# Decode tokens of a hybrid decoder layer: outputs from the old recurrent state, new state made in a later stage

## The chip, the cores and the metric

One core of one Trainium2 chip runs the whole step. The metric is device time in microseconds (us) of one execution; the figure to compare is the median of three runs.

## The reference

One decoder layer is applied to a prompt of 1024 tokens and to 8 decode tokens (one new token for each of 8 sequences). Both go through a half-step SwiGLU feed-forward, then attention heads beside Mamba-2 heads, an output projection, cross attention into 256 memory tokens, a second half-step feed-forward and a final norm. The part that matters here is the Mamba-2 recurrence of a decode token. For every sequence, head and channel, with the old state h0 (128 numbers per channel), it computes

```
h = exp(dt * a) * h0 + dt * x * B        # 16 heads x 64 channels x 128, an output
y = sum over n of C[n] * h[n] + d_skip * x
```

All of h (8 x 16 x 64 x 128 floats, 4 MB) is an output, and y goes on through the gate, the group norm and the output projection of the same layer. B and C are shared by the 8 heads of a group; there are two groups.

## The kernel before

Activations lie with features on the 128 partitions and the 1032 tokens along the free dimension. Matrix products are made of three fp32r products of a high and a low part. Tensors come from pools of slots by tag: a tile waits until its slot is free, which is when the last user of the tile that held it, a DMA included, is done. The order of instructions on each engine comes from a scheduler, which walks the program with a cost model and takes, for each engine, the first instruction in program order that is ready; so an instruction can run far ahead of its place in the program, and its order against others is fixed before the run. Nearly all DMAs are issued by one in-order queue, SyncE's (SPq).

The stages are, in order of time in the profile: first feed-forward (to about 860 us), attention with the input projections as filler (to 1310), the scan (1310 to 1545), the output projection (to 1640), cross attention (1640 to 1860), the last projection and preparation (to 1965), second feed-forward.

In the scan, `ssd(g, c)` (L1200) handles chunk c of group g of the prompt: it loads a 128 x 1024 row block `bc` (L1206), takes exponentials on ScalarE (L1210, L1212, L1217), multiplies on VectorE (L1227) and GpSimd (L1229, L1240, L1258), multiplies on TensorE (L1241, L1250) and adds the state on VectorE (L1259). Beside it run the z projections (`pzz`), the first half of the output projection (`wout_o`, L1368: load 344 columns, multiply, add, store back), gates and splits (`gate_split`, L1295). The decode tokens have their place between the chunks. `dec_conv(g)` (L1308) makes x, B, C and dt * x; `dec_ssm(g, b0)` (L1335) handles two sequences; `dec_out(g)` (L1353) adds the skip term and copies the result to the last 8 columns. In `dec_ssm`, a pair of states `sv` sits in one slot of the tag "hb", which has three slots and is shared with `bc`; `t1` is a PSUM bank (PS) of the pair that `pst` of `ssd` uses too.

Cross attention is `cross_q(h)` (query projection, TensorE), `cross_att(h)` (prompt) and `cross_dec(h)` (decode tokens, with 8 loads of 512 KB of cached keys and values per head) for four heads; `cross_in` loads back stored outputs, and from L1672 the last projection `pco` runs as filler. `sq_` and `acc_` are rings of 4 and 3 slots of 388 columns (tags "tu" and "ts").

Of the kernel before, what the change touches and what calls it, by code (L numbers as in the profile page):

```python
# [10 lines left out]
F32 = mybir.dt.float32  # L11
F32R = mybir.dt.float32r
I32 = mybir.dt.int32
AF = mybir.ActivationFunctionType
OP = mybir.AluOpType
# [4 lines left out]
NDEC = 8  # L20
# [56 lines left out]
def tile_step(ctx, tc, a, o):  # L77
    nc = tc.nc
    pool = lambda **kw: ctx.enter_context(tc.tile_pool(**kw))
    cp = pool(name="consts", bufs=1)  # L80
# [5 lines left out]
    st = {}  # L86
# [23 lines left out]
    sq_, acc_, g1_, u1_ = ring("tu", 4, PA), ring("ts", 3, PA), ring("tg", 2, PA), ring("tv", 2, 344)  # L110
# [33 lines left out]
    def PS(name="ps"):  # L144
        return st["pair"].tile(list(st["shape"]), F32, name=name, tag="s", bufs=st["bufs"])
# [717 lines left out]
    def conv_block(m):  # L863
# [7 lines left out]
        def ev(p, s, n):  # L871
# [15 lines left out]
            def rows():  # L887
                q = PD("pcv")
                nc.tensor.transpose(q[:11, :128], tail, ident)
                cvo = tq.tile([16, 128], F32, name="cvo", tag="cvo", bufs=1)[:11]  # L890
                nc.scalar.copy(cvo, q[:11, :128])
                nc.sync.dma_start(o[4][0, 0][:, m * 128:(m + 1) * 128], cvo[0:3])
                nc.sync.dma_start(o[10][0, :, 2, m * 128:(m + 1) * 128], cvo[3:11])
# [37 lines left out]
    for t0, n in TGS:  # L931
        s = slice(t0, t0 + n)
        p = PD("pdt")
# [370 lines left out]
    ct = mp.tile([128, 6, NDEC], F32, name="ct")  # L1304
    dtx = [mp.tile([128, 4, NDEC], F32, name=f"dtx{g}") for g in range(2)]
    yd = [mp.tile([128, 4, NDEC], F32, name=f"yd{g}") for g in range(2)]

    def dec_conv(g):  # L1308

# [22 lines left out]
        nc.vector.tensor_copy(bcT, flat(p)[:8, :256])  # L1332
        nc.sync.dma_start(bc_scr[g], bcT)

    def dec_ssm(g, b0):  # L1335

        sv = H("hb", "sv")[:, :1024].rearrange("p (b j n) -> p b j n", b=2, n=128)
        hs = slice(g * 8, g * 8 + 8)
        for u in range(2):
            b = b0 + u  # L1340
            nc.sync.dma_start(sv[:, u], a["state_ssm"][0, b, hs].rearrange("(j e) p n -> (e p) j n", e=2))
            bb = acc_()[:, :256]
            nc.sync.dma_start(bb, bc_scr[g, b:b + 1].broadcast_to([128, 256]))
            t1 = PS("pt1").rearrange("p (j n) -> p j n", n=128)
            for j in range(4):
                nc.scalar.activation(t1[:, j], bb[:, :128], AF.Copy, scale=dtx[g][:, j, b:b + 1])
                nc.scalar.activation(sv[:, u, j], sv[:, u, j], AF.Copy, scale=ddb[:, 1, g * 4 + j, b:b + 1])
            nc.vector.tensor_add(sv[:, u], sv[:, u], t1)
            nc.vector.tensor_mul(t1, sv[:, u], bb[:, None, 128:].to_broadcast([128, 4, 128]))
            nc.vector.tensor_reduce(yd[g][:, :, b], t1, mybir.AxisListType.X, OP.add)  # L1350
            nc.sync.dma_start(o[11][0, b, hs].rearrange("(j e) p n -> (e p) j n", e=2), sv[:, u])

    def dec_out(g):  # L1353
        nc.vector.tensor_mul(dtx[g], xcd[:, g, 0:4], dsk[:, g * 4:g * 4 + 4, None].to_broadcast([128, 4, NDEC]))
        nc.vector.tensor_add(yd[g], yd[g], dtx[g])
        for j in range(4):
            nc.vector.tensor_copy(xc[4 * g + j][:, SEQ:T], yd[g][:, j])
# [286 lines left out]

    cross_q(0)
    cross_q(1)
    cross_att(0)
    cross_dec(0)
    cross_q(2)
    cross_att(1)  # L1650
    cross_dec(1)
    cross_q(3)
    for k in range(4):
        cross_in(k)
    acts[4:] = [(A("coh"), A("col")) for _ in range(4)]
    cross_dec(2)
    cross_att(2)
    cross_dec(3)
    cross_att(3)
    wco = lambda half, m: w_co[half * 512:half * 512 + 512].rearrange("(k p) n -> p k n", p=128)[:, :, m * 128:(m + 1) * 128]  # L1660
    x = [None] * KD

# [174 lines left out]
```

## Time and profile before

| what | value |
| --- | --- |
| median of three runs | 2673.5 us (2665.6 to 2675.37) |
| the profiled execution | 2677.61 us, of it 2675.8 us from its first to its last instruction |
| VectorE, ScalarE, GpSimd busy | 67%, 44%, 34% of the span |
| mean granted TensorE clock | 0.972 of full speed |
| HBM | 204.25 MB read, 49.98 MB written |

TensorE is busy nearly throughout. A stage is judged by how far TensorE falls short in it and by what TensorE then waits for; the averages over the span say little about a stage.

### The profile page before, as it was taken

Reading aid. Unit: us, or ns where it says so; the run is one execution under the profiler, and the core shown is the slowest. Engines: PE = TensorE matmul, PEld = TensorE weight load, DVE = VectorE, ACT = ScalarE, POOL = GpSimd, SP = SyncE. Lnnn points to the kernel's source line nnn. Section 1 sums busy time; section 2 is a strip of 40 time slices with the busy share of each in tenths; the row PEclk is TensorE's granted clock in tenths of the full one; section 3 lists DMA queues with packets and bytes.
Section 4 is the critical chain, followed back from the end, with each engine's and each line's share of the span. In section 5 each row is a group of like instructions: output and inputs, shape, how many; then the busy total and the mean of one; then the engine's idle time right before and its main releaser. Section 6 shows DMA issues by size and latency. Waiting matters only on the chain.

```text
span 2675.8 us, 42135 instructions
## 1 busy us (share of the span) xinstructions
PE 2517.3 (94%) x15999; PEld 2391.8 (89%) x15999; DVE 1797.9 (67%) x3648; ACT 1172.5 (44%) x2413; POOL 911.8 (34%) x687
## 2 busy tenths in 40 slices
PE   6899999999999999999897899989889999999998
PEld 5899999999998899999686798879789999999997
DVE  7566666666667676778578867565686666666665
ACT  5433333333334455554477523232443333333345
POOL 5433333333325111115265664101643333333333
PEclk9999999999999999999898999999999999999999
DMA  5411211112113222227666634573111111111112
GB/s 171 136 49 57 62 60 57 57 57 64 57 48 105 75 69 78 87 74 236 199 196 221 211 94 134 170 219 116 34 48 48 48 48 49 55 48 51 53 48 80
DMA packets 273748, 252.13 MB, mean 94 GB/s; under 512 B 17392, under 2 KB 243880, under 8 KB 273536
## 3 DMA queue, kind: packets, MB, share of 16 engines
q1 hardware_dynamic: 271872, 249.34, 30.3%
q8 instruction: 126, 2.06, 0.3%
q14 instruction: 78, 0.64, 0.1%
q10 hardware_dynamic: 1672, 0.09, 0.0%
HBM read 204.25 MB, written 49.98 MB: 95 GB/s over the span
## 4 chain that ended last, share of the span: by engine, by line
PE 69%; DVE 14%; DMA 8%; issue 3%; ACT 3%; POOL 2%; SPq 0%; DVEq 0%; ACTq 0%; POOLq 0%
PE fb L319 44%; PE pqkv L255 5%; PE pxbc L255 4%; PE pcq L255 2%; PE pco L255 2%; DMA fraw<-in_w_up_dram 2%; PE pwa L255 2%; PE po L1061 1%; DVE fs L353 1%; PE ps L1035 1%; PE ptr L1055 1%; PE pzz L255 1%; DMA cqb<-cq_scr 1%; DVE ckv L1531 1%; DMA kb<-in_cache_win_k_dram 1%
## 5 line engine op out<-in xcount | busy, mean ns | idle before, releaser
L245 POOL TENSOR_TENSOR wl<-wr,wh 128x1024 fp32r<-128x1024 f32 (+4 forms) x79 | 165.5, 2095 | 569.9 <-ACT wh L241 542.4
L307 POOL TENSOR_TENSOR fw<-fraw,fw 128x512 fp32r<-128x512 f32 x131 | 174.7, 1333 | 467.4 <-ACT fw L306 387.8
L307 POOL TENSOR_TENSOR fw<-fs,fw 128x512 fp32r<-128x512 f32 x128 | 172.5, 1348 | 398.6 <-ACT fw L306 351.0
L306 ACT CAST fw<-fs 128x512 fp32r<-128x512 f32 x256 | 158.2, 618 | 272.6 <-PE fb L319 161.3
L306 ACT CAST fw<-fraw 128x512 fp32r<-128x512 f32 x262 | 162.2, 619 | 186.2 <-PE fb L319 182.2
L353 DVE TENSOR_TENSOR fs<-fraw 128x512 f32<-128x512 f32 (+1 forms) x168 | 103.4, 615 | 136.0 <-DMA fraw<-in_w_up_dram 67.3
L307 DVE TENSOR_TENSOR fw<-fraw,fw 128x512 fp32r<-128x512 f32 x131 | 102.2, 780 | 113.0 <-ACT fw L306 113.0
L307 DVE TENSOR_TENSOR fw<-fs,fw 128x512 fp32r<-128x512 f32 x128 | 96.2, 752 | 94.4 <-ACT fw L306 94.4
L319 PE MATMUL fb<-hRh,fw 128*128 128x256 f32 x640 | 137.3, 280 | 0.4
L241 ACT CAST wh<-wr 128x1024 fp32r<-128x1024 f32 (+1 forms) x80 | 76.8, 960 | 117.8 <-PE pwa L255 29.7
L319 PEld LDWEIGHTS fb<-hRh,fw 128*128 128x128 f32 x640 | 109.2, 188 | 3.6 <-DVE x L505 3.6
L255 PE MATMUL pxbc<-xh,wh 128*128 128x344 f32 x288 | 94.0, 326 | 2.0 <-DVE xr L872 2.0
L255 PE MATMUL pqkv<-xh,wh 128*128 128x344 f32 x288 | 93.8, 326 | 0.3 <-DVE x L535 0.3
L255 PE MATMUL pxbc<-xl,wh 128*128 128x344 f32 x288 | 93.5, 325 | 0.0
L255 PE MATMUL pqkv<-xh,wl 128*128 128x344 f32 x288 | 93.1, 323 | 0.0
L255 PE MATMUL pqkv<-xl,wh 128*128 128x344 f32 x288 | 92.9, 323 | 0.0
L255 PE MATMUL pxbc<-xh,wl 128*128 128x344 f32 x288 | 92.9, 323 | 0.0
L319 PE MATMUL fb<-hRl,fw 128*128 128x256 f32 x320 | 87.7, 278 | 0.0
L398 DVE TENSOR_TENSOR tu<-fb,ts 128x388 f32<-128x388 f32 x44 | 24.7, 562 | 90.2 <-ACT ts L395 90.2
L1042 ACT ACTIVATE pr<-pr,nm 128x128 f32<-128x128 f32 (+3 forms) x64 | 49.7, 777 | 55.3 <-DVE nm L1040 55.0
L319 PE MATMUL fb<-T2h,fw 128*128 128x388 f32 x160 | 54.2, 359 | 18.7 <-ACT fb L488 18.7
L1040 DVE CUSTOM_DVE_ANT_0 pr<-ps,U 128x128 f32<-128x128 f32 (+3 forms) x64 | 48.1, 751 | 27.2 <-PE ps L1035 16.9
(806 smaller groups left out, 9420.3 us busy)
## 6 DMA issues: line engine op xcount, KB each, us to landing
fraw<-in_w_gate_dram SPq DMA_DIRECT2D x44, 512.0 KB
fraw<-in_w_up_dram SPq DMA_DIRECT2D x44, 512.0 KB
fraw<-in_w_down_dram SPq DMA_DIRECT2D x44, 512.0 KB
wr<-in_w_in_dram SPq DMA_DIRECT2D x32, 512.0 KB
x_scr<-x SPq DMA_DIRECT2D x16, 516.0 KB
x<-x_scr SPq DMA_DIRECT2D x16, 516.0 KB
bc<-acs_scr SPq DMA_DIRECT2D x16, 512.0 KB
ckv<-in_cache_mem_k_dram SPq DMA_DIRECT2D x16, 512.0 KB
```

What stands on the lines that cost most here:

```text
L241: nc.scalar.copy(hi[:, :w], raw[:, :w])
L245: e.tensor_sub(lo[:, q], raw[:, q], hi[:, q].bitcast(F32))
L255: nc.tensor.matmul(ps, w, v, start=i == 0, stop=i == last)
L306: nc.scalar.copy(hi, src)
L307: (nc.vector if st["turn"] else nc.gpsimd).tensor_sub(lo, src, hi.bitcast(F32))
L319: nc.tensor.matmul(ps, l[:, js], m, start=bool(start and not i), stop=bool(stop and i == 2), skip_group_check=True)
L353: nc.vector.tensor_tensor(dst, t[p], t[q], op=op)
L1035: ins = nc.tensor.matmul(ps[:, c:c + n], qs[:, b * 128:w], kk[:, c:c + n], start=i == 0, stop=i == 1)
L1040: nc.vector.tensor_tensor_reduce(pr[:, :w], ps[:, :w], U[:, 896 - b * 128:1024], -1.0, 3e38, OP.add, OP.min, nm)
L1042: nc.scalar.activation(pr[:, :w], pr[:, :w], AF.Exp, scale=-1.0, bias=nm, accum_out=sm)
L1055: nc.tensor.transpose(p[:, j], pr[:, (c + j) * 128:(c + j + 1) * 128], ident)
L1061: nc.tensor.matmul(po[:, b % 2].rearrange("p i t -> p (i t)"), vv[:, j, e].rearrange("p i d -> p (i d)"), tts[j // 4][:, j % 4].rearrange( ...
```

## The change

`dec_ssm` no longer makes the new state. It multiplies the loaded old state by C on GpSimd, in place, sums over n on VectorE, and takes the product B.C of each token with one more VectorE instruction. `dec_out` then scales these sums by exp(dt * a) and adds (dt * x) * (B.C); it also keeps copies of dt * x and exp(dt * a) that outlive the scan. A new function, `dec_state(g, b)`, loads the old state of one sequence a second time, loads B, makes h on ScalarE and GpSimd and stores it; sixteen calls of it are placed between the calls of the cross attention. A small tile, `cvo`, moves from a slot of its own to the ring "tu".

```diff
-                cvo = tq.tile([16, 128], F32, name="cvo", tag="cvo", bufs=1)[:11]
+                cvo = sq_(128)[:11]
...
+    dab = cp.tile([128, 8, NDEC], F32, name="dab")
+    dtb_ = [cp.tile([128, 4, NDEC], F32, name=f"dtb{g}") for g in range(2)]
...
+    bC = [mp.tile([128, NDEC], F32, name=f"bC{g}") for g in range(2)]
+    rows8 = lambda t, g, b: t[0, b, g * 8:g * 8 + 8].rearrange("(j e) p n -> (e p) j n", e=2)
+
     def dec_ssm(g, b0):
 
         sv = H("hb", "sv")[:, :1024].rearrange("p (b j n) -> p b j n", b=2, n=128)
-        hs = slice(g * 8, g * 8 + 8)
         for u in range(2):
             b = b0 + u
-            nc.sync.dma_start(sv[:, u], a["state_ssm"][0, b, hs].rearrange("(j e) p n -> (e p) j n", e=2))
+            nc.sync.dma_start(sv[:, u], rows8(a["state_ssm"], g, b))
             bb = acc_()[:, :256]
             nc.sync.dma_start(bb, bc_scr[g, b:b + 1].broadcast_to([128, 256]))
-            t1 = PS("pt1").rearrange("p (j n) -> p j n", n=128)
-            for j in range(4):
-                nc.scalar.activation(t1[:, j], bb[:, :128], AF.Copy, scale=dtx[g][:, j, b:b + 1])
-                nc.scalar.activation(sv[:, u, j], sv[:, u, j], AF.Copy, scale=ddb[:, 1, g * 4 + j, b:b + 1])
-            nc.vector.tensor_add(sv[:, u], sv[:, u], t1)
-            nc.vector.tensor_mul(t1, sv[:, u], bb[:, None, 128:].to_broadcast([128, 4, 128]))
-            nc.vector.tensor_reduce(yd[g][:, :, b], t1, mybir.AxisListType.X, OP.add)
-            nc.sync.dma_start(o[11][0, b, hs].rearrange("(j e) p n -> (e p) j n", e=2), sv[:, u])
+            nc.gpsimd.tensor_mul(sv[:, u], sv[:, u], bb[:, None, 128:].to_broadcast([128, 4, 128]))
+            nc.vector.tensor_reduce(yd[g][:, :, b], sv[:, u], mybir.AxisListType.X, OP.add)
+            nc.vector.tensor_tensor_reduce(bb[:, :128], bb[:, :128], bb[:, 128:], 1.0, 0.0, OP.mult, OP.add, bC[g][:, b:b + 1])
+
+    def dec_state(g, b):
+
+        sv = st["cq"].tile([128, 512], F32, name="sv", tag="sv", bufs=2).rearrange("p (j n) -> p j n", n=128)
+        nc.sync.dma_start(sv, rows8(a["state_ssm"], g, b))
+        bb = acc_()[:, :128]
+        nc.sync.dma_start(bb, bc_scr[g, b:b + 1, :128].broadcast_to([128, 128]))
+        for j in range(4):
+            nc.scalar.activation(sv[:, j], sv[:, j], AF.Copy, scale=dab[:, g * 4 + j, b:b + 1])
+        for h in range(2):
+            t1 = sq_()[:, :256].rearrange("p (j n) -> p j n", n=128)
+            for j in range(2):
+                nc.scalar.activation(t1[:, j], bb, AF.Copy, scale=dtb_[g][:, 2 * h + j, b:b + 1])
+            nc.gpsimd.tensor_add(sv[:, 2 * h:2 * h + 2], sv[:, 2 * h:2 * h + 2], t1)
+        nc.sync.dma_start(rows8(o[11], g, b), sv)
 
     def dec_out(g):
+        nc.vector.tensor_mul(yd[g], yd[g], ddb[:, 1, g * 4:g * 4 + 4])
+        nc.vector.tensor_copy(dtb_[g], dtx[g])
+        nc.vector.tensor_copy(dab[:, g * 4:g * 4 + 4], ddb[:, 1, g * 4:g * 4 + 4])
+        nc.vector.tensor_mul(dtx[g], dtx[g], bC[g][:, None, :].to_broadcast([128, 4, NDEC]))
+        nc.vector.tensor_add(yd[g], yd[g], dtx[g])
...
     cross_q(0)
     cross_q(1)
+    dec_state(0, 0)
     cross_att(0)
+    dec_state(0, 1)
+    dec_state(0, 2)
     cross_dec(0)
+    dec_state(0, 3)
+    dec_state(0, 4)
     cross_q(2)
+    dec_state(0, 5)
     cross_att(1)
+    dec_state(0, 6)
+    dec_state(0, 7)
     cross_dec(1)
+    dec_state(1, 0)
     cross_q(3)
+    dec_state(1, 1)
     for k in range(4):
         cross_in(k)
     acts[4:] = [(A("coh"), A("col")) for _ in range(4)]
     cross_dec(2)
+    dec_state(1, 2)
     cross_att(2)
+    dec_state(1, 3)
+    dec_state(1, 4)
     cross_dec(3)
+    dec_state(1, 5)
     cross_att(3)
+    dec_state(1, 6)
+    dec_state(1, 7)
```

## Rows read from the trace of the kernel before

**Rows 1.** The head of the page: each engine's busy time over the span, with its share and its number of instructions.

```profile
PE 2517.3 (94%) x15999; PEld 2391.8 (89%) x15999; DVE 1797.9 (67%) x3648; ACT 1172.5 (44%) x2413; POOL 911.8 (34%) x687
```

**Rows 2.** Busy time by stage: start and end (us), length, then busy us of TensorE, its weight loads, VectorE, ScalarE and GpSimd with their instructions, the granted clock, the DMA engines' busy share and GB/s. The stages are the scan, its second part, the cross attention, and a piece of that.

```profile
1310.00:1545.00 235.00, 207.55 (x1395) 168.15 (x1396) 178.54 (x391) 150.37 (x395) 124.40 (x96) 0.91 0.69 215
1400.00:1545.00 145.00, 119.15 (x829) 105.13 (x828) 126.46 (x259) 94.60 (x243) 85.15 (x66) 0.90 0.68 212
1640.00:1860.00 220.00, 207.57 (x1343) 187.64 (x1342) 124.56 (x389) 67.87 (x157) 26.20 (x15) 0.97 0.55 171
1757.00:1800.00 43.00, 35.02 (x230) 28.10 (x222) 27.66 (x83) 18.52 (x41) 0.00 (x0) 0.92 0.82 258
```

**Rows 3.** Waits in the scan (1310 to 1545): who waited for whom, us in total, times, longest. The first three rows are the longest of TensorE's fourteen, then one row each of ScalarE and VectorE.

```profile
PE pcb L1221 <- DVE tg L1238: 4.4, 1, 4.4
PE pst L1241 <- DVE yd L1350: 4.2, 3, 3.7
PE pwo L255 <- DVE ol L1434: 3.9, 2, 2.1
...
ACT sv L1347 <- DMA sv<-in_state_ssm_dram: 15.1, 6, 5.2
...
DVE dcy L1215 <- DMA bc<-acs_scr: 12.1, 7, 3.4
```

**Rows 4.** The chain that ended last in the scan: its shares of the window by engine and line, then pieces of it in order of time (start us, us, what).

```profile
by line: PE pzz L255 10.4%; PE pod L1168 7.3%; DMA bc<-acs_scr 7.3%; issue 6.5%; DMA out_dram<-sv 4.9%; PE py L1250 4.3%; DVE yl L1300 4.2%; DMA x_scr<-tu 4.0%; DMA sv<-in_state_ssm_dram 3.6%; PE pst L1241 3.2%; DVE pt L1349 3.0%; ACT E L12
...
1427.66 5.18 DMA out_dram<-sv
...
1488.33 6.45 DMA out_dram<-sv
1494.84 5.25 DMA bc<-acs_scr
```

**Rows 5.** Groups of instructions in the scan by line: busy us and mean ns of one, then the engine's idle time before them and what ended it.

```profile
L1346 ACT ACTIVATE pt<-ts,dtx 128x128 f32<-128x128 f32 x64 | 21.7, 363 | 6.4 <-DVE hn L1259 5.2 <-PE py L1250 0.8
...
L1300 DVE SCALAR_TENSOR_TENSOR yl<-xs,gv,yh 128x344 fp32r<-128x344 f32 x20 | 20.6, 1052 | 0.0
...
L1347 ACT ACTIVATE sv<-sv,ddb 128x128 f32<-128x128 f32 x64 | 20.1, 389 | 24.3 <-DMA sv<-in_state_ssm_dram 15.1 <-POOL tv L1240 9.2
...
L1258 POOL TENSOR_TENSOR hn<-hn,cd 128x512 f32<-128x512 f32 x14 | 16.9, 1209 | 5.5 <-ACT hn L1261 4.9 <-DVE hn L1259 0.7
...
L1349 DVE TENSOR_TENSOR pt<-sv,ts 128x512 f32<-128x512 f32 x16 | 15.9, 1002 | 0.1
...
L1348 DVE TENSOR_TENSOR sv<-sv,pt 128x512 f32<-128x512 f32 x16 | 10.7, 682 | 5.6 <-ACT pt L1346 5.6
```

**Rows 6.** Single lines of the kernel over the whole span: engine, operation, count, then ns of one (least, median, most), first and last start.

```profile
L1349 DVE TENSOR_TENSOR pt<-sv,ts x16: 686/700/2529, 1350.9 to 1538.4; 128x512 f32<-128x512 f32 x16
L1300 DVE SCALAR_TENSOR_TENSOR yl<-xs,gv,yh x24: 562/718/2689, 1451.2 to 1563.4; 128x344 fp32r<-128x344 f32 x24
L1355 DVE TENSOR_TENSOR yd<-yd,dtx x2: 180/186/191, 1431.1 to 1542.3; 128x32 f32<-128x32 f32 x2
L1531 DVE CUSTOM_DVE_ANT_0 ckv<-ckv,cqb x64: 403/422/2557, 1677.9 to 1816.0; 128x256 f32<-128x256 f32 x64
L1531 DVE DVE_READ_ACCUMULATOR2_ANT csc<- x64: 70/83/86, 1678.3 to 1816.3; 128x1 f32 x64
L1240 POOL TENSOR_TENSOR tv<-tg,dcy x32: 608/616/1593, 1330.1 to 1524.7; 128x256 f32<-128x256 f32 x32
```

**Rows 7.** Instructions of GpSimd and VectorE in order of time around 1402 us (start us, us, engine, line).

```profile
1402.11 2.38 POOL L245 TENSOR_TENSOR wl<-wr,wh 128x1024 fp32r<-128x1024 f32 x1
1402.51 2.53 DVE L1349 TENSOR_TENSOR pt<-sv,ts 128x512 f32<-128x512 f32 x1
```

**Rows 8.** SyncE's queue in order of time, the life of one pair of states, and ScalarE's eight operations on one later pair.

```profile
1361.19 0.99 SPq L1341 DMA_DIRECT2D sv<-in_state_ssm_dram  x2
...
1377.22 0.99 SPq L1351 DMA_DIRECT2D out_dram<-sv  x2
...
1389.35 2.43 ACT L1347 ACTIVATE sv<-sv,ddb 128x128 f32<-128x128 f32 x8
```

**Rows 9.** The DMA view: packets, bytes and mean rate in the scan, then the same in the cross attention with the size of one issue of the state's load in the scan, and the busy tenths in 40 slices of 1757 to 1800.

```profile
DMA packets 42930, 50.58 MB, mean 215 GB/s; under 512 B 3460, under 2 KB 36356, under 8 KB 42907
...
sv<-in_state_ssm_dram SPq DMA_DIRECT2D x16, 256.0 KB
...
DMA packets 34604, 37.54 MB, mean 171 GB/s; under 512 B 1920, under 2 KB 30874, under 8 KB 34586
...
DMA  0596004979967989999878989989998899996857
```

**Rows 10.** Waits in the cross attention (1640 to 1860): the longest of TensorE's ten, and the longest two of SyncE's queue.

```profile
PE pcs L1535 <- DVE csc L1531: 3.0, 3, 2.2
...
SPq L239 <- POOL wl L245: 57.3, 11, 11.8
SPq L1522 <- DVE csc L1531: 34.3, 12, 4.9
```

**Rows 11.** The longest load on the chain in the cross attention (start us, us, what), and ScalarE's group of the attention stage (900 to 1240) that writes the ring "tu".

```profile
1786.16 7.80 DMA ckv<-in_cache_mem_v_dram
...
L1007 ACT COPY tu<-pkv 128x256 f32<-128x256 f32 x32 | 10.5, 375 | 14.2 <-PE pkv L1003 9.4 <-DMA out_dram<-tu 4.2 <-ACT tu L1007 0.5
```

## The prediction, made before the changed kernel had run

> **What bounds the kernel now.** I read the page's head first: TensorE is busy 94% of the span, VectorE 67%, GpSimd 34% [rows 1]. So time can only come from stages in which TensorE falls short, and I took busy time by stage next [rows 2]. In the scan TensorE is busy 207.55 of 235 us, so 27.5 us are idle, and its granted clock is 0.91, a mix of the two levels 2.4 and 1.2 GHz. In the cross attention it is idle 220 - 207.57 = 12.4 us, at 0.97. VectorE is busy 126.46 of 145 us, 87%, in the second part of the scan, ScalarE 65%, GpSimd 59%. In the cross attention ScalarE is idle 152 us and GpSimd 194.
>
> The waits come third [rows 3]: TensorE's three longest in the scan are all for VectorE (4.4, 4.2 and 3.9 us), and the second of them, `pst` for the reduction L1350, is the PSUM bank that `t1` shares. ScalarE waits 15.1 us for the loads of states, with the exponentials of the chunks queued behind it. Last the chain [rows 4]: from about 1375 us on it hardly runs over TensorE. Two stores of states stand on it (5.18 and 6.45 us), and right behind the second one a load of `bc` (5.25 us): the load needed the "hb" slot that the store held. A pair's load is issued at 1361.19 and its two stores at 1377.22 [rows 8]; with a store's 5 to 6 us the pair holds one of three slots for 22 us.
>
> So the scan's second part is bound by VectorE and by the three slots, both of which the decode tokens use.
>
> **The change, part by part.**
>
> Scan, VectorE. The add L1348 and the multiply L1349 go: 10.7 + 15.9 = 26.6 us [rows 5]. The reductions stay. Sixteen B.C products come: no row has 128 x 128, but the same operation on 128 x 256 takes 422 ns and 83 for its accumulator [rows 6], 505 in all; a tiny instruction takes 186 and an accumulator 83, 269 in all. I take 400 ns, 6.4 us in sum. Five small instructions per group come at 0.19 [rows 6], 1.9 us. And GpSimd takes over the multiplication: 16 x 1.21 us by L1258 of the same shape [rows 5], 19.3 us. While GpSimd works, VectorE is held up at times: L1349 took 2.53 us while a GpSimd instruction of 2.38 us ran, against a median of 0.70 [rows 6, 7]. The surplus of means over undisturbed ones is 16 x 0.30 for L1349 and 20 x (1.052 - 0.562) for L1300 [rows 5, 6], 14.6 us beside 124.4 us of GpSimd [rows 2], 0.12 per us; so 19.3 us more of GpSimd cost VectorE about 2.3. The sum is -26.6 + 6.4 + 1.9 + 2.3 = -16.0 us. The sixteen are spread from 1351 to 1538 us [rows 6], so 74% of it, 11.8 us, falls where VectorE is 87% busy.
>
> The Trainium skill, page "SBUF — State Buffer", section "Who interferes with whom", says more sharply that a VectorE instruction with two SBUF inputs and a GpSimd instruction that reads SBUF exclude each other for the whole instruction, and that a reduction never does. The trace agrees with the first for L1349 [rows 7]; how often it bites is decided by the order in time. That rule speaks against the change (third rival).
>
> Scan, other engines. ScalarE loses 128 instructions at 2.43/8 = 0.304 us [rows 8], 39 us of 150, and with them the wait for the load; that wait moves to GpSimd, behind whose multiply L1240, L1229 and L1258 of the chunks are queued, for which `pst`, `py` and the new state wait. SyncE's queue loses 16 stores with their waits, DMA 16 x 256 KB = 4.2 of 50.6 MB [rows 9]. A slot is freed after load, two multiplies and a reduction, 5 + 2 x 1.2 + 0.7 = about 8 us instead of 22.
>
> Scan, sum. By the chain, the stores (4.9%) and L1349 (3.0%) of 235 us go, 18.6 us [rows 4]; by VectorE's work 11.8. At the worst GpSimd's multiplies stand before a chunk's own every second time, 8 x 1.2 = 10 us lost. I take a gain of 14, between the first two, nearer to VectorE's, because next late are the `bc` load itself (7.3% of the chain), the store and reload of `x_scr` (4.0%) and `yl` (4.2%), which stay. `dec_out` adds its five instructions, 1 us, on the path to the last gate; this is in it.
>
> Cross attention, DMA. Each of 16 calls moves 256 KB in, 64 KB of B (128 rows of 512 B) and 256 KB out: 9.4 MB on 37.5 [rows 9]. The DMA engines were busy 0.55 x 220 = 121 us for 37.5 MB, 3.2 us per MB, so 30 us are added and the share becomes 0.69, which the scan has now. Only 1757 to 1800 is full: share 0.82 [rows 2], most slices at 8 or 9 tenths [rows 9], TensorE idle 8 us of 43. Spread evenly, 16 x 43/220 = 3.1 calls fall there, 1.9 us each: 6 us if each is paid, none if the scheduler runs them ahead. I take 2.
>
> Cross attention, engines. ScalarE gets 128 x 0.304 = 39 us into 152 idle ones, in lumps of four (1.2 us) ahead of exponentials, and waits for the loads as it does now in the scan, about 15 us in all; with TensorE's ten waits there so short (the longest 3.0 us in all [rows 10]) I take 1. GpSimd gets 32 x 0.616 = 19.7 us [rows 6] into 194 idle, ahead of the low parts of weights: 1. SyncE's queue gets 48 issues of about 0.5 us [rows 8], 24 us. It stands waiting at least 57.3 + 34.3 us [rows 10], so it has room, but each store waits at its head for a GpSimd addition, with loads of cached keys and of weights behind: 1. Sum 5; ends 0 (nothing is taken out of this stage) and 20 (last rival).
>
> `cvo` moves into the ring "tu". ScalarE's 32 copies into it waited 4.2 us in all for stores [rows 11]; 12 more users cost 0 to 4 us, and TensorE has projections to do meanwhile: 0.
>
> **Sum.** 2677.6 - 14 + 5 = 2668.6 us for the profiled execution. Its time was 4.1 us above the median of 2673.5, so 2664.5 against that median.
>
> **Rivals.**
>
> *The slots give more.* With a pair gone after 8 us, `bc` is loaded a chunk ahead, and its loads (7.3%, 17 us) leave the chain too [rows 4]. For it: VectorE waits 12.1 us for `bc` [rows 3]. Against: VectorE's other work is still there. Scan -25, cross +1: 2649.5.
>
> *GpSimd gives it back.* If each multiply holds VectorE for its 1.21 us, 19.3 instead of 2.3 us are added, and VectorE's sum is +1.0. Then only slot and stores help, 5 us, and the cross costs 4: 2672.5. For it: rows 7. Against: 14.6 us of such loss beside 124 us of GpSimd today. By the rule of the Trainium skill on that page this is how each overlap would end.
>
> *Slower: the queue in the cross attention.* There the chain already holds a 7.80 us load of cached values [rows 11]. If a state's store waits at the head of SyncE's queue, with the load of keys behind it, and this happens for 12 of 16 calls at 1.2 us (a lump of four on ScalarE) and 3 pay their transfers at 1.9, that is 20 us. With only 3 gained in the scan the result is +17: 2690.5. It decides once TensorE's idle time in that stage passes 12.4 + 14 us. Against: of ScalarE's 152 idle us 98 and of GpSimd's 194 some 174 would still be left.
>
> That the states might still be made in the scan is excluded: their slots are in the cross attention's pool.
>
> **Chances.** A change within 0.5%, 13.4 us, is what a measurement of this kernel can hardly tell from none; so faster is below 2660.1 and slower above 2686.9. The forecast has 0.50, its own range 2654 to 2675; the bigger gain 0.20, the give-back 0.17, slower 0.13. A third of the forecast's chance lies below 2660.1: faster 0.17 + 0.20 = 0.37; slower 0.12 (a little of that case ends below its bound); same 0.51. The range of 8 in 10 reaches into both ends, 2646 to 2684.
>
> **What would show it.** Right: VectorE's busy time in the scan falls by 10 to 18 us, no store of states on the chain there, the scan about 14 us shorter; TensorE's idle time in the cross attention 15 to 20 us. Wrong: L1300 and the multiply of `cbm` (L1227) grow longer with GpSimd; the chunks' GpSimd work waits for loads of states; the cross attention grows by more than 10 us, with the queue waiting for additions of states.

## The result, and the profile after

The changed kernel takes 2699.86 us (median of 6 runs, 2692.59 to 2706.65); the kernel before, beside it, 2669.47 (2665.19 to 2675.37). The ratio is 1.0117, with a 95% interval of 1.0101 to 1.0134. It is slower, by 30.4 us between the medians; the prediction was 2664.5, with a range that ended at 2684. The profiled executions lie closer together, 2692.59 and 2677.61 us: that of the changed kernel was the fastest of its six, that of the kernel before one 8 us above its median, with a first feed-forward 6.5 us longer than in the changed kernel's, where nothing was changed.

The head of the changed kernel's page answers to [rows 1]: busy us of each engine, its share of the span, instructions.

```profile
PE 2522.0 (94%) x15999; PEld 2395.3 (89%) x15999; DVE 1811.1 (67%) x3658; ACT 1170.8 (44%) x2413; POOL 964.7 (36%) x735
```

VectorE was to lose work and has 13.2 us more (1797.9 before); GpSimd has 52.9 more. Where the time went is seen by cutting both traces at the same instructions. I took the first start of four products: `pdt` (the attention begins), `pcc` (the first transposes of `dec_conv`, the scan begins), `pwb` (the first half of the weights of the output projection that wait for the scan; the cross attention follows behind it) and `pco` with the late weights `cw` (the last projection). What lies ahead of `pdt` (876.4 us before, 869.9 after, 861.3 to 876.4 over all kernels below) was touched by none of the edits and is left out. First the kernel before, then the changed one, the three stretches between these points in the view of busy time by window; the last row of the second fence is the cross attention alone, as in [rows 2].

```profile
876.40:1312.30 435.90, 415.16 (x2734) 400.83 (x2734) 328.41 (x670) 226.74 (x434) 94.11 (x42) 0.97 0.37 108
1312.30:1586.20 273.90, 248.00 (x1657) 208.56 (x1658) 200.69 (x433) 157.91 (x407) 154.93 (x124) 0.93 0.63 195
1586.20:1869.30 283.10, 266.42 (x1700) 244.41 (x1700) 176.36 (x463) 95.52 (x212) 62.07 (x43) 0.97 0.50 156
```

```profile
869.90:1318.40 448.50, 417.36 (x2735) 401.79 (x2734) 332.40 (x672) 225.69 (x434) 97.45 (x42) 0.97 0.35 107
1318.40:1588.40 270.00, 244.91 (x1657) 205.48 (x1658) 204.51 (x441) 120.35 (x279) 178.25 (x140) 0.93 0.60 180
1588.40:1883.40 295.00, 270.16 (x1700) 247.48 (x1700) 182.86 (x463) 133.23 (x340) 85.69 (x75) 0.95 0.58 182
...
1641.00:1874.00 233.00, 212.61 (x1343) 192.04 (x1344) 132.11 (x390) 105.60 (x285) 50.79 (x47) 0.94 0.66 203
```

The attention is 12.6 us longer, the scan 3.9 shorter, the stretch with the cross attention 11.9 longer. What comes behind is the same (806.5 and 807.3 us). So two stretches lost, and one of them holds nothing of the change but the move of `cvo`. In the scan VectorE is busy 3.8 us more than before, although an add and a multiply of 26.6 us [rows 5] are gone. (Two more kernels below have the old scan, in other orders of work; VectorE is busy 204.9 and 204.3 us there, so 200.7 is the least of three.)

In the cross attention TensorE is idle 20.4 us of 233 (12.4 of 220 in [rows 2]), and its granted clock, a mix of the levels 2.4 and 1.2 GHz, fell from 0.97 to 0.94, so that the same products took 5.0 us longer; the 13.0 us that this piece is longer are these two. All sixteen states ran in its first 100 us: the trace shows the loads of `dec_state` from 1640.7 to 1726.7 us and its stores from 1650.1 to 1736.9. These are the waits there, TensorE's against [rows 10], then SyncE's queue, ScalarE and GpSimd at the states (us in total, times, longest).

```profile
PE pcs L1554 <- DVE csc L1550: 5.4, 4, 2.1
PE cpod L1574 <- DMA ckv<-in_cache_mem_v_dram: 4.4, 3, 1.8
PE pq L1529 <- DVE q L1524: 3.7, 1, 3.7
PE cps L1619 <- ACT qh L1609: 3.6, 1, 3.6
...
SPq L1355 <- DMA out_dram<-sv: 16.0, 10, 3.7
SPq L1365 <- POOL sv L1364: 13.1, 9, 2.3
SPq L1365 <- DMA sv<-in_state_ssm_dram: 6.9, 3, 4.1
...
ACT sv L1359 <- DMA sv<-in_state_ssm_dram: 10.8, 7, 4.3
```

For the last two of TensorE's rows, `pq` and `cps`, it can be followed in time what stood behind a wait on an engine that works in order. Rows of ScalarE, TensorE, SyncE's queue, VectorE and GpSimd of the changed kernel around these two gaps, each engine's in order of time (start us, us, engine, line; in brackets the idle time before and what ended it):

```profile
1669.57 0.98 ACT L1359 ACTIVATE sv<-sv,dab 128x128 f32<-128x128 f32 x3 [2.00 <-DMA sv<-in_state_ssm_dram]
1670.46 0.60 ACT L1609 CAST qh<-q 128x512 fp32r<-128x512 f32 x1
...
1671.12 0.58 PE L1619 MATMUL cps<-mh,qh 128*128 128x256 f32 x1 [3.56 <-ACT qh L1609]
...
1682.36 0.38 SPq L1355 DMA_DIRECT2D sv<-in_state_ssm_dram  x1
1682.83 0.45 SPq L1546 DMA_DIRECT2D cqb<-cq_scr  x1
...
1688.23 0.82 DVE L1550 CUSTOM_DVE_ANT_0 ckv<-ckv,cqb 128x256 f32<-128x256 f32 x1 [4.94 <-DMA ts<-bc_scr]
...
1691.26 2.55 DVE L1550 CUSTOM_DVE_ANT_0 ckv<-ckv,cqb 128x256 f32<-128x256 f32 x1
...
1694.60 0.93 DVE L1524 SCALAR_TENSOR_TENSOR q<-pcq,r 128x344 f32<-128x344 f32 x2
...
1695.16 0.27 PE L1529 MATMUL pq<-ident,q 128*8 128x128 f32 x1 [3.65 <-DVE q L1524]
...
1691.10 2.42 POOL L245 TENSOR_TENSOR wl<-wr,wh 128x1024 fp32r<-128x1024 f32 x1
```

The first gap: ScalarE stood 2.0 us for the load of a state, and the cast of queries that TensorE needed was behind three scalings of that state. The second: VectorE stood 4.9 us before its product of keys, with the reading of the projection's bank (L1524) behind it. The row names a load of B, which this instruction doesn't read; it reads `cqb`, which was issued at 1682.83, right behind the load of a state, so `cqb` is the likelier end of that wait. And one of these products took 2.55 us instead of 0.42, while GpSimd was at a low part of weights until 1693.52.

### The profile page after: what moved, and what is told of

Read it like the earlier page. It is cut to its first block, busy times and chain, and to the rows that moved or that the text cites. A ratio compares the mean times of both kernels' runs of the same rounds, so it can differ in the third digit from the quotient of the medians.

```text
span 2690.7 us, 42260 instructions
## 1 busy us (share of the span) xinstructions
PE 2522.0 (94%) x15999; PEld 2395.3 (89%) x15999; DVE 1811.1 (67%) x3658; ACT 1170.8 (44%) x2413; POOL 964.7 (36%) x735
## 5 line engine op out<-in xcount | busy, mean ns | idle before, releaser
L1040 DVE CUSTOM_DVE_ANT_0 pr<-ps,U 128x128 f32<-128x128 f32 (+3 forms) x64 | 48.0, 749 | 31.4 <-PE ptr L1055 14.8
```

Source lines behind the costliest of these rows:

```text
L1040: nc.vector.tensor_tensor_reduce(pr[:, :w], ps[:, :w], U[:, 896 - b * 128:1024], -1.0, 3e38, OP.add, OP.min, nm)
```

## The experiments

Thirteen kernels ran. For all of them, the ratio to the kernel before on the same chip, with its 95% interval, and the three stretches of the profiled execution. Line numbers in rows are each kernel's own.

| kernel | what it is | ratio | attention | scan | cross attention |
| --- | --- | --- | --- | --- | --- |
| before | | 1 | 435.9 | 273.9 | 283.1 |
| after | the change | 1.0117 (1.0101 to 1.0134) | 448.5 | 270.0 | 295.0 |
| e1_ring | before, with `cvo` in the ring | 1.0077 (1.0047 to 1.0107) | 446.6 | 279.9 | 277.0 |
| e2_own_slot | after, with `cvo` in its own slot | 1.0065 (1.0047 to 1.0083) | 435.2 | 274.0 | 293.5 |
| e3_no_state | e2 without the new states | 1.0002 (0.9985 to 1.0019) | 433.6 | 277.8 | 278.3 |
| e4_state_twice | before, and the states made a second time | 1.0066 (1.0049 to 1.0084) | 438.1 | 270.6 | 294.3 |
| e5_mul_vector | e3, multiplication on VectorE | 0.9982 (0.9962 to 1.0001) | 436.4 | 268.8 | 279.3 |
| e6_no_mul | e3 without the multiplication | 0.9967 (0.9952 to 0.9983) | 434.8 | 264.4 | 282.0 |
| e7_state_dma | e2, of the states the transfers alone | 1.0030 (1.0013 to 1.0047) | 437.1 | 276.6 | 291.5 |
| e8_no_store | e2, states not stored | 1.0033 (1.0017 to 1.0050) | 434.2 | 273.8 | 291.7 |
| e9_pool_queue | e2, states' transfers on GpSimd's queue | 1.0057 (1.0038 to 1.0076) | 437.9 | 273.2 | 293.0 |
| e10_paced | e2, states spread over the stage | 1.0040 (1.0023 to 1.0057) | 435.6 | 275.5 | 290.6 |
| e11_states_ffn2 | e5, states in the second feed-forward | 1.0014 (1.0003 to 1.0024) | 437.2 | 267.5 | 280.4 |
| e12_state_arith | e2, of the states the arithmetic alone | 1.0032 (1.0017 to 1.0048) | 435.5 | 276.3 | 284.7 |
| e13_ffn2_vector | e11 without GpSimd | 0.9998 (0.9986 to 1.0010) | 435.9 | 268.6 | 276.7 |

A stretch is of one execution. The eight kernels with the changed scan and GpSimd's multiplication have 270.0 to 277.8 us there, so a difference of some 4 us between two single stretches says nothing, and with the old scan, which ran in three different orders of work, it is 9 us (270.6 to 279.9). The means over alike kernels say more, and the ratios, but alike kernels are not independent: seven of the eight have the very same order of VectorE's instructions in the scan, the changed kernel has another, and e5, e11 and e13 share a third. A mean over them evens out the execution, not the order.

**The three parts one by one.** Four kernels first. e1_ring is the kernel before with one line changed:

```diff
-                cvo = tq.tile([16, 128], F32, name="cvo", tag="cvo", bufs=1)[:11]
+                cvo = sq_(128)[:11]
```

> The kernel before, with one line of the change alone: the tile cvo (L890) moves from its own slot to the ring tu. Between the two profiles the attention stage, from the first matmul of pdt (L936) to the first of pcc (the start of the decode tokens' convolution), is 12.4 us longer after the change (448.5 against 436.1 us), although nothing else of the change stands in it. Theory A (this line reorders the stage): the stage is 446 to 450 us here and the whole kernel 0.3% to 0.6% slower, ratio 1.003 to 1.006. Theory B (the attention stage differs because of the parts of the change that come behind it, or by chance of the execution): the stage is 434 to 439 us and the ratio 0.998 to 1.002.

e2_own_slot is the changed kernel with that line as it was (and the two small tiles `bC` in another pool, to make room for the slot).

> The changed kernel with cvo in its own slot again (the small tiles bC move to the scan's own pool, which makes the room). Theory A: the attention stage is back at 434 to 439 us, and the kernel about 12 us faster than the changed one, ratio to the kernel before 1.005 to 1.008. Theory B: the ratio stays at 1.010 to 1.013, the stage at 446 to 450 us. In both the stretch from the first pwb matmul to the first matmul on cw (cross attention) stays near 295 us, against 283 before.

e3_no_state takes out of e2 the sixteen calls:

```diff
-    dec_state(0, 0)
...
-    dec_state(1, 7)
```

> As e2_own_slot, without the sixteen calls that make the new state: the new state of the decode tokens is neither made nor stored, so this is the scan's part of the change alone. Theory C (the scan gives little, since GpSimd takes over what VectorE loses): from the first pcc matmul to the first pwb matmul 268 to 272 us against 273.9 before, the cross attention stretch 281 to 285, ratio 0.997 to 1.000. Theory D (my forecast's gain of 14 us is there, and was hidden by the order of that one profile): 258 to 262 us, ratio 0.993 to 0.996.

e4_state_twice keeps the scan of the kernel before and adds the sixteen calls, which store to a scratch tensor.

> The kernel before, scan untouched, plus the sixteen calls in the cross attention: the new state is made a second time from a second load and stored to a scratch tensor. Theory E (the calls themselves lengthen the cross attention): from the first pwb matmul to the first matmul on cw 292 to 300 us against 283, ratio 1.003 to 1.007. Theory F (the stage is longer because the changed scan hands over in another order): 281 to 287 us, ratio 1.000 to 1.002.

The ring costs 0.77% by e1_ring (four runs, interval 0.47% to 1.07%; more than the 0.3% to 0.6% expected) and 0.52% by the changed kernel against e2. In the attention it is 11.6 us, 0.43% (446.6 and 448.5 us with the ring, 433.6 to 438.1 without); no stretch shows the rest of e1_ring's 0.77%. The states cost 0.63% (e2 against e3) or 0.66% (e4), in the cross attention. The scan gives nothing that can be told: e3 has all of the scan's lighter work and is at 1.0002, just above theory C's 0.997 to 1.000, with 277.8 us in the scan where C had 268 to 272.

How can a tile of 0.5 KB per partition cost 10 us? These are TensorE's waits in the attention, first of the changed kernel, then of e1_ring; in the kernel before the same two were 1.9 and 2.0 us.

```profile
PE ps L1035 <- DVE nm L1040: 7.6, 6, 2.3
PE pxbc L255 <- DVE xr L872: 6.7, 3, 5.0
```

```profile
PE pxbc L255 <- DVE xr L872: 7.2, 3, 4.9
PE ps L1035 <- DVE nm L1040: 7.1, 6, 2.3
```

Neither `nm` nor `xr` has anything to do with `cvo` or its ring. What differs is the order. TensorE's products in e1_ring and in the kernel before are the same ones in the same order for the first 5783 of 15,999; then, in the attention, five products `po` and the scores `ps` stand earlier among the projection `pxbc`, and from there on the order differs to the end of the stage. The changed kernel has nearly e1_ring's order there, the kernels without the ring nearly that of the kernel before. The likely reason, which no run singles out, is that the scheduler saw a tile that has to wait for one of four shared slots. So the price is mainly that of another order, not of waits for slots: ScalarE's copies into the ring waited 7.8 us for stores in the changed kernel, 6.6 in e1_ring and 4.2 before [rows 11], while the two waits above grew by 10.4 us.

**Why the scan gives nothing.** e5 and e6 are e3 with one line moved or gone:

```diff
-            nc.gpsimd.tensor_mul(sv[:, u], sv[:, u], bb[:, None, 128:].to_broadcast([128, 4, 128]))
+            nc.vector.tensor_mul(sv[:, u], sv[:, u], bb[:, None, 128:].to_broadcast([128, 4, 128]))
```

> e3_no_state with the multiplication of the old state by C back on VectorE; the new state is not made here either. Theory A (GpSimd's multiplications hold VectorE up): between the first transposes of dec_conv and the first products of wout_a (278 us in e3_no_state) VectorE was busy 223.5 us there and 220.4 before, though 26.6 us of its work went and 13 came; the rest is hold-ups by the 21.6 us of GpSimd. So VectorE takes 16 x 0.7 to 1.0 = 11 to 16 us back and loses some 17 of hold-ups: busy 217 to 224, the copy of cd (550 ns there, 164 before) back under 250 ns, the time 2655 to 2668 us. Rival B (GpSimd holds nothing up; VectorE's longer instructions have another cause): VectorE 235 to 240 us, the copy of cd still near 550, the time 2668 to 2680.

> e3_no_state with the multiplication of the old state by C left out, so the tokens' outputs are sums of the old state alone, and the new state is not made. Shows what the scan can give at most by lighter decode tokens. Theory A (VectorE, with the hold-ups, paces the scan): VectorE busy 202 to 208 us in that stretch, the stretch 6 to 14 us shorter than 278, the time 2650 to 2659. Rival B (TensorE, its granted clock and the loads pace the stretch; decode tokens are off its path): VectorE's busy time falls just the same, the stretch stays at 274 to 279, the time 2662 to 2669.

Busy time in the scan, of e3, e5 and e6 (VectorE is the third of the five sums, GpSimd the fifth); e3's second row is its cross attention, for further down.

```profile
1300.40:1578.20 277.80, 246.48 (x1656) 206.60 (x1657) 207.10 (x441) 119.91 (x279) 176.93 (x140) 0.94 0.56 177
1578.20:1856.50 278.30, 263.62 (x1702) 241.51 (x1701) 176.52 (x463) 95.30 (x212) 61.89 (x43) 0.98 0.51 159
```

```profile
1301.40:1570.20 268.80, 247.40 (x1657) 206.46 (x1658) 205.59 (x457) 120.61 (x279) 158.06 (x124) 0.93 0.59 183
```

```profile
1308.80:1573.20 264.40, 244.12 (x1656) 202.39 (x1657) 195.16 (x442) 120.26 (x279) 156.09 (x124) 0.96 0.58 186
```

(The expectations count by sums over the groups of lines, where instructions that overlap count twice; by that count e3 has 225.7, e5 226.0 and e6 214.0, and the 223.5 given there is the changed kernel's. The windows count them once.) VectorE is busy 195.2 us without the multiplication, 205.6 when it makes it itself and 207.1 when GpSimd makes it. So GpSimd's multiplication, 176.9 - 156.1 = 20.8 us, cost VectorE 11.9 us of standing, about as much as the 10.4 that the same work takes on VectorE: over all kernels VectorE is busy 204.5 to 208.0 us with it on GpSimd and 205.6 to 207.2 with it on VectorE. That is 0.57 us for each us; I had reckoned 0.12. The orders of e3 and e6 differ too, so some of the 11.9 can be order.

The time is a weaker witness. e5 is at 0.9982 and e3 at 1.0002, with intervals that overlap; the stretch is 268.3 us as the mean of three kernels with VectorE's multiplication (e5, e11, e13) against 274.7 as the mean of eight with GpSimd's. VectorE's busy time, the same in both, can't be what shortens it; TensorE is idle less (21.4 us in e5, 31.3 in e3), and whether the place of the multiplication or the order does that isn't shown. Of theory A the times are in its ranges and the copy of `cd` is back at 164 ns in the median; VectorE's sums came out above the 217 to 224 and 202 to 208 that I gave, and in e5 the sum didn't fall at all. And e6 is the ceiling of the idea in the order that it got: without any multiplication the kernel is only 0.33% (8.8 us) faster.

How an instruction is held is seen in e3, GpSimd and VectorE in order of time around 1375 us:

```profile
1373.64 2.37 POOL L1229 TENSOR_TENSOR bc<-bc,bc 128x1024 f32<-128x1024 f32 x1
1375.96 2.39 POOL L245 TENSOR_TENSOR wl<-wr,wh 128x1024 fp32r<-128x1024 f32 x1
...
1373.91 2.24 DVE L1350 CUSTOM_DVE_ANT_0 ts<-ts 128x128 f32<-128x128 f32 x1 [2.21 <-DMA ts<-bc_scr]
1376.08 0.08 DVE L1350 DVE_READ_ACCUMULATOR2_ANT bC<- 128x1 f32 x1
1376.19 2.20 DVE L1371 TENSOR_TENSOR dtx<-dtx,bC 128x32 f32<-128x32 f32 x1
```

The product B.C ends at 1376.15, just after GpSimd's instruction (1376.01); the next, of 32 elements to a partition, at 1378.39, just after GpSimd's next one (1378.35). Where nothing held them they took 0.28 and 0.17 us. Of the instructions that went, one was of the other kind: the add L1348 of the kernel before took one input from PSUM and was 0.68 us each time, though a GpSimd instruction ran beside 12 of the 16. So the change took away one instruction that wasn't held and one that was (L1349 of the kernel before), and put in the product B.C and small ones in `dec_out` that can be. Nor does a hold-up vanish with the instruction that had it: in e6, where the multiplication isn't there at all, the small difference L1215 was 601 ns in the mean, 338 in the kernel before, and the product with `cbm` L1227 1612 against 1366. GpSimd's other 156 us are there in all of them, and can hold whichever two-input instruction stands there. The rule of the Trainium skill, page "SBUF — State Buffer", section "Who interferes with whom", says that a VectorE instruction with two inputs in SBUF and a GpSimd instruction that reads SBUF exclude each other for a whole instruction; the trace agrees, with 2.24 and 2.20 us here and 0.68 for the add. How often that happens is a matter of the order.

**What the states pay for in the cross attention.** e7 keeps of `dec_state` only its three transfers, e8 all but the store, e12 only the arithmetic:

```diff
-        for j in range(4):
-            nc.scalar.activation(sv[:, j], sv[:, j], AF.Copy, scale=dab[:, g * 4 + j, b:b + 1])
...
-            nc.gpsimd.tensor_add(sv[:, 2 * h:2 * h + 2], sv[:, 2 * h:2 * h + 2], t1)
```

> e2_own_slot with only the transfers of dec_state: load of the state, load of B, store of the same slot; the instructions of ScalarE and GpSimd are left out, so the old state is stored as the new one. The 16 calls cost 0.63% (16.8 us) by e2_own_slot against e3_no_state. Theory A (transfers and the places they take in SyncE's queue cost it: a load waits for the store of the slot before it, keys and weights wait behind): 2676 to 2682, at least 0.4% over before. Rival B (work on ScalarE and GpSimd, or stores that wait for it at the head of the queue, cost it): 2665 to 2671, 0.2% over before at the most.

> e2_own_slot with the stores of dec_state left out, loads and arithmetic kept; the new state is made and not written. Theory A (the load of a state waits for the store of two calls before at the head of the queue; stores are half the price or more): 2666 to 2672, less than half of the 16.8 us is left. Rival B (arithmetic and loads cost it, with ScalarE's copies and the wait for their load): 2674 to 2681.

> e2_own_slot with the transfers of dec_state left out but for the first two loads: the 128 instructions on ScalarE and 32 on GpSimd work over and over on two tiles that stay, with a constant tile in the place of B; the new state is not stored. Left of the price so far: all 0.65%, transfers alone 0.30%, loads and arithmetic without stores 0.33%. Theory A (the parts add up: arithmetic, in front of other work on ScalarE and with GpSimd holding VectorE up, costs what transfers alone don't): 1.0025 to 1.0045, 2671 to 2677 us, VectorE in the cross attention 5 to 8 us longer than the 176.5 of e3_no_state. Rival B (arithmetic costs something only where it waits for loads, and others wait behind it): 0.9995 to 1.0015, 2664 to 2669 us.

Transfers alone cost 0.30%, arithmetic alone 0.32%, both 0.65%: by the ratios the parts add up, 8 us each, as theory A of e12 had it. For e7 neither theory fits (less than A's 0.4%, more than B's 0.2%). e8's 2674.39 us lies at the lower end of rival B's range and outside theory A's. So with the arithmetic left out half of the price is gone, and with the stores left out half is gone. The stretches divide it otherwise, 12 us in e7, 12 in e8 and 5 in e12 over the 279.5 without states; each is of one execution, so halves is as far as this can be told. Busy time in the cross attention, of e2 and then of e12; e3's row stands above.

```profile
1574.20:1867.70 293.50, 271.69 (x1701) 249.21 (x1700) 182.03 (x463) 133.20 (x340) 85.38 (x75) 0.95 0.59 183
```

```profile
1582.20:1866.90 284.70, 265.26 (x1702) 241.83 (x1701) 188.53 (x463) 131.76 (x340) 85.53 (x75) 0.98 0.50 157
```

From e3 to e2 TensorE's busy time grows by 8.1 us and its idle time by 7.1 (14.7 to 21.8). The same products at a clock of 0.95 in place of 0.98 are 263.62 x 0.98 / 0.95 = 271.9 us, so the busy half of the price is the granted clock. In the first 40 us of the states it was 0.90 in e2 and 0.96 in e3:

```profile
1627.70:1667.70 40.00, 37.29 (x222) 36.59 (x223) 20.76 (x63) 27.50 (x80) 16.71 (x17) 0.90 0.73 215
1631.70:1671.70 40.00, 39.76 (x254) 39.44 (x253) 21.69 (x81) 9.86 (x18) 6.41 (x3) 0.96 0.42 129
```

Over the whole stretch it was at its lower level, 1.2 GHz, for 30.7 us in e2 and 10.2 in e3, each time during or soon behind a gap of TensorE of 1.7 to 3.2 us; but not every gap brought a fall (the 3.65 us before `pq` in the changed kernel did not). With the arithmetic alone the clock stays at 0.98, but VectorE grows by 12.0 us, above the 5 to 8 expected; with the transfers alone VectorE stays at 176.8, which points to GpSimd's additions as what holds it.

How transfers alone get at TensorE is seen in e7. Its longest gap, in order of time by engine:

```profile
1673.79 3.24 SPq L1358 DMA_DIRECT2D out_dram<-sv  x2
1677.14 0.35 SPq L1525 DMA_DIRECT2D cq_scr<-cqd  x1
1679.01 1.04 SPq L1355 DMA_DIRECT2D sv<-in_state_ssm_dram  x2
1680.09 0.50 SPq L1539 DMA_DIRECT2D cqb<-cq_scr  x1
...
1686.04 0.43 DVE L1543 CUSTOM_DVE_ANT_0 ckv<-ckv,cqb 128x256 f32<-128x256 f32 x1 [16.73 <-DMA cqb<-cq_scr]
...
1688.81 0.93 DVE L1517 SCALAR_TENSOR_TENSOR q<-pcq,r 128x344 f32<-128x344 f32 x2
...
1689.38 0.38 PE L1522 MATMUL pq<-ident,q 128*8 128x128 f32 x1 [11.97 <-DVE q L1517]
1689.41 0.64 PE L255 MATMUL pcq<-xh,wh 128*128 128x344 f32 x1
```

VectorE had copied the queries at 1665.6; the queue issued their store at 1677.14, 11.5 us later, behind loads and stores of states (in e3 it was 0.03 us later). The reload follows behind two more loads of states, at 1680.09. VectorE's order has the first product of keys at its head, so it stands 16.7 us for that reload, with the reading of a bank behind it, and TensorE stands 12.0 us for the bank. When it starts again a product takes 0.49 us for some 5 us, at a granted clock of 0.50, where it took 0.32.

**Another queue, another pace, another stage.**

```diff
-        nc.sync.dma_start(sv, rows8(a["state_ssm"], g, b))
+        nc.gpsimd.dma_start(sv, rows8(a["state_ssm"], g, b))
```

> e2_own_slot with the 48 transfers of the 16 dec_state calls issued by GpSimd's queue instead of SyncE's; all is computed. Theory A (the price in the cross attention is order in in-order queues: loads of queries, keys, values and weights stand in SyncE's queue behind loads and stores of states): half or more of the 0.65% goes, 2665 to 2674 us, and TensorE no longer waits several us for DVE q or for ACT qh. Rival B (the price is the 9.4 MB themselves, as the DMA engines are shared by all queues): 2677 to 2684. Rival C (GpSimd now stands waiting for free slots, with its low parts of weights behind): over 2684, with TensorE waiting for POOL wl.

e10 calls `dec_state` behind each pair of loads of cached rows and ties its transfers to them:

```diff
+            with tc.issue_after(st["ck"]):
+                dec_state(h // 2, h % 2 * 4 + b0 // 2)
```

> e2_own_slot with each dec_state call's transfers held behind two of the 32 loads of cached keys and values, so that the states are spread over the whole stage and don't run ahead in its first 100 us; all is computed. Theory A (the price comes from the lump of 16 states in the first 100 us, ahead of loads that TensorE needs): 2668 to 2675 us. Rival B (every state costs its price wherever it stands in this stage, as its loads and stores stand before keys and queries all the same): 2677 to 2684. Rival C (spread, they fall into the last part, where the loads of cached rows alone fill the DMA engines): over 2684.

GpSimd's queue gives nothing that can be told (1.0057 against 1.0065): theory A falls, and the time, 2678.96 us, is in rival B's range. SyncE's queue by itself is not the price. The Trainium skill, page "DMA: Bandwidth & Descriptors", section "Issuing engines are not separate DMA queues", says that all queues run on the same 16 DMA engines; the trace agrees as far as it goes: their share in that stretch is 0.59 in both. The gaps were others: at `pq` TensorE stood 0.7 us instead of 2.8, but twice, 3.65 and 3.05 us, for `csc`. Pacing seems to give some of it (1.0040, interval to 1.0057, against 1.0065, interval from 1.0047; 2673.49 us, within theory A's range but near its end); the states ran from 1635 to 1840 us there. So the lump is at most a part of the price.

e11 makes the states in the second feed-forward, in halves of two heads, with the scan of e5; e13 is e11 with ScalarE and VectorE doing what GpSimd did:

```diff
+        if 2 <= m < 18:
+            with tc.issue_after(st["load"]):
+                for h in range(2):
+                    dec_state((m - 2) // 8, (m - 2) % 8, h)
```

```diff
-            nc.scalar.activation(t1[:, j], bb, AF.Copy, scale=dtb_[g][:, 2 * h + j, b:b + 1])
-        nc.gpsimd.tensor_add(sv, sv, t1)
+            nc.vector.scalar_tensor_tensor(sv[:, j], bb, dtb_[g][:, 2 * h + j, b:b + 1], sv[:, j], op0=OP.mult, op1=OP.add)
```

> e5_mul_vector (tokens' outputs from the old state, multiplication on VectorE) with the new states made in the second feed-forward, in halves of two heads, one sequence per block of 128 hidden features, each transfer behind that block's weight loads; all is computed. In the kernel before, the DMA share there is 0.17 and ScalarE is busy 39%, in the cross attention 0.55 and 31%. Theory A (the states cost what they displace in in-order queues; where loads are early and the share is low they cost next to nothing): 2655 to 2664 us, ratio 0.996 to 1.000. Rival B (making them costs something anywhere, by ScalarE's and GpSimd's instructions in front of work for TensorE): 2668 to 2680.

> e11_states_ffn2 without GpSimd: h is made by ScalarE's scaling and one VectorE instruction per head (B times dt * x plus the scaled state), in place; all is computed. In e11_states_ffn2 TensorE waits in the second feed-forward for VectorE's additions into x 10.6 us in all between 2000 and 2500 us, 3.7 before. Theory A (GpSimd's additions hold VectorE up there too, and that is the price of 8 us): 2659 to 2665 us, ratio 0.9975 to 1.0000. Rival B (VectorE's own new work, 64 instructions of some 0.3 us, delays the additions into x just as much): 2666 to 2671, ratio 1.0005 to 1.0025.

e11 came out at 1.0014 and 2668.26 us, beyond theory A's range and at the lower end of rival B's; what follows the cross attention took 812.9 us, against 804.7 in e5. TensorE's waits for VectorE from 2000 to 2500 us, of e11 and then of e13:

```profile
PE fb L319 <- DVE x L490: 6.3, 8, 0.8
PE fb L319 <- DVE x L496: 4.3, 8, 0.5
```

```profile
PE fb L319 <- DVE x L496: 4.3, 8, 0.5
```

With GpSimd out of it the first wait is gone, the stretch is at 803.6 us and the ratio at 0.9998, the top of theory A's range. That is the best complete version: as fast as the kernel before, not faster. Whether the scan of e5 gives 0.2% (0.9962 to 1.0001) that the states take again, these intervals can't tell.

## Why the prediction was wrong

The forecast was -14 in the scan, +5 in the cross attention, 0 for the ring. By the means over alike kernels the stretches say 0 (274.7 us against 274.8), +14.8 (294.3 with all states run as written, 279.5 without) and +11.6 (447.6 against 436.0). The sum is +26.4, against a measured difference of the medians of 30.4; the 4 us between are not placed.

*The scan's sum for VectorE.* The removal of 26.6 us was right. Wrong was "14.6 us beside 124.4 us of GpSimd, 0.12 per us; so 19.3 us more of GpSimd cost VectorE about 2.3". This is the step that failed, in two ways. The average was of two groups of lines. Taken over all of VectorE's instructions in the stretch, the time above the shortest instruction of the same kind in any of these traces is 48.8 us in the kernel before, 0.31 per us of GpSimd, and all but 3 us of it in instructions that ran beside one of GpSimd's; it is 66.2 in the changed kernel, 68.9 in e3 and 57.6 in e6. And an average is not the price of more: that was 11.9 us for 20.8. The rest of the miss has nothing to do with the multiplication. Without any (e6) VectorE is busy 5.5 us less than before, where -26.6 + 6.4 + 1.9 gives 18.3 less, and the stretch is 9.5 us shorter, not 14. New two-input instructions, the products B.C and the small ones of `dec_out`, can be held where the add that went couldn't; I priced them undisturbed, 0.40 and 0.19 us, and in the changed kernel the products B.C took 0.91 in the mean. And the surplus that I took from L1349 as belonging to it stayed when it went. VectorE ended with 3.8 us more in the stretch, not 16.0 less, and the row that I had named as the sign, VectorE's busy time falling by 10 to 18 us, says so. The rival "GpSimd gives it back" was right in its mechanism and near in its sum of +1.0 for VectorE.

*Slots and stores.* As predicted, no store of a state stands on the scan's chain any more. Nothing came of it: ScalarE's exponentials waited 29.1 us for loads of `bc` (11.2 before), and VectorE had no less to do.

*The cross attention's +5.* DMA at 2, ScalarE, GpSimd and SyncE's queue at 1 each were together too small: TensorE's idle time grew by 8.0 us, and its products by 5.0 us with the lower granted clock, for which the sum has no term. The reasoning that failed is that I asked whether an engine has idle time to spare; in an in-order list it matters who stands behind the wait. The "slower" rival had the place, the mechanism of a queue and a price of 20 near the 14.8 measured, yet it named SyncE's queue; the runs show no single queue at fault, as the price halves without the transfers and halves without the arithmetic, and stays on another queue. That its time of 2690.5 is the nearest to the measured 2699.86 is luck: the ring, which it didn't contain, brought it there. Its point of decision, TensorE's idle time beyond 26.4 us in that stage, was not reached (20.4): the other part came through the granted clock. Of the signs given, the cross attention growing by over 10 us and the queue waiting for additions of states (13.1 us) came. L1227 grew (from 1366 to 1466 ns), but it also did in e6, without the multiplication; L1300 didn't (1055 to 903). GpSimd waited 6.0 us for the loads of its multiplications, and VectorE 2.8 us for the products: that sign came, but small.

*The ring.* "12 more users cost 0 to 4 us" priced waits for slots. The step that failed is the bound: it takes the order of the work as given, and the order is made anew for every program. That line alone moved the attention by 11.6 us and the time by 0.5% to 0.8%.

Open stays how much of the 11.6 us is this one order's bad luck: another small edit might as well fall on a better one, and no run tried a second. The same holds for the scan: the old one spread over 9 us in three orders, seven executions of one order of the new one over 5.

## What to carry to other kernels

When work moves from one engine to another, do not price what the receiving engine does to its neighbours by an average over a few lines: take the surplus of all instructions that can be held, and the full overlap as the bound (here 2.3 us by the average, 19.3 by full overlap, 11.9 measured); ask of each instruction that goes and comes whether it is one that can be held. Idle time of an engine is no room for work with waits in it: look at what stands behind the wait in that engine's list, and give such work a place where its loads are early, as in the feed-forward here. Where a scheduler writes the order, no edit is local: run the "harmless" line by itself.

## What the hardware showed that was not expected

A VectorE instruction of 32 elements to a partition took 2.20 us, ending just after the GpSimd instruction that it met, and one of 128 elements 2.24; so what a hold-up costs doesn't go by the size of the instruction held. Moving a multiplication from VectorE to GpSimd cost VectorE about as much standing (11.9 us) as it saved it work (10.4). And half of the cross attention's price in e2 is not idle time but TensorE's products running longer, at a granted clock of 0.95 against 0.98: 8.1 us, beside 7.1 of gaps.
